# Two weight sums of a pair made by the transfers that load them, and 26 feed-forward pairs in the wide form

## The chip, the cores and the metric

The kernel runs on one core of a Trainium2 chip. The metric is the time of one execution in device microseconds; several runs are given by their median.

## The reference

One decoder layer on 512 tokens of width 1024, all in float32: a SwiGLU feed-forward, a mixer that merges dilated window attention with a linear recurrence, and a second SwiGLU feed-forward. Root-mean-square norms stand around each. What the change touches are the products of the inputs with the gate and up weights of the feed-forwards, and with weights of the mixer's input projection.

```python
def swiglu(x, w_gate, w_up, w_down):
    return (jax.nn.silu(x @ w_gate) * (x @ w_up)) @ w_down

for l in range(DEPTH):                       # DEPTH = 1
    f = swiglu(rms_norm(h, ffn1_norm_pre[l]), ffn1_w_gate[l], ffn1_w_up[l], ffn1_w_down[l])
    h = h + 0.5 * rms_norm(f, ffn1_norm_post[l])
    u = rms_norm(h, mix_norm_pre[l])
    proj = u @ w_in[l]
    q, k, v, xr, yr, gl = jnp.split(proj, splits, axis=-1)
    ...
    h = h + rms_norm(merged @ w_out[l], mix_norm_post[l])
    f = swiglu(rms_norm(h, ffn2_norm_pre[l]), ffn2_w_gate[l], ffn2_w_up[l], ffn2_w_down[l])
    h = h + 0.5 * rms_norm(f, ffn2_norm_post[l])
```

The feed-forward width is 2816, which is 22 blocks of 128 columns. There are 12 attention heads of width 128, in three groups of four.

## The kernel before

**Split products.** TensorE takes its operands in a reduced float format (`F32R`). The kernel keeps the precision by splitting each operand into a high part, rounded, and a low part, the rest, and by adding three products: high by high, high by low, low by high. `split` (L302, L303) makes both parts of a tile: a copy on ScalarE writes the high part, a subtraction on VectorE the low one. Weights arrive in `raw` tiles (128 x 1024, four buffers) by transfers on the SP queue, in one fixed stream (`stream_plan`); their split parts go to `w8` tiles (four buffers) and `w4` tiles (two).

**Pairs.** Two blocks of 128 output columns, gate and up of one block f in a feed-forward or a query and a key block in attention, make a pair. A pair has four quarters of weights: g0, g1 (gate, first and second half of the 1024 rows) and u0, u1 (up). It is computed with seven products instead of eight, in the manner of Strassen and Winograd, over the two halves of the rows and the two halves of the tokens. The input's forms are made once per stage (`x_forms`, `forms_of`). The weights' forms are made per pair by `w_forms`: four adds of 128 x 512 on VectorE (L691, L692, L693, L696) and four splits, three of 1024 columns (tiles a, b, c) and one of 512 (d). The sums are

- s2 = u0 + u1 (for p5), s1 = u0 + u1 + g0 (for p6), u0 + g0 (for p7) and u0 + u1 + g0 + g1 (for p3); g0, g1 and u1 themselves serve p1, p2 and p4.

In this kernel tile a holds p1 and p2, tile b (from the tile `s12`, tag `s`, two buffers) p6 and p5, tile c p7 and p4.

**Three ways to run the seven products.** Each product is a sum over four blocks of 128 rows.

- `seven_on` (narrow, L729 to L731): three matmuls of 256 columns for each block, high by high, high by low, low by high, all into one 256-column area. Partial results are copied by ScalarE from one bank to the next and added by VectorE from the banks.
- `seven` is a variant of it for the first pairs of a feed-forward.
- `seven_wide` (L779, L780): the high weight is loaded once and multiplied with high and low input side by side, 512 columns; the low weight then multiplies the high input, 256 columns, into the second half. The result stands in two halves of a bank. Moves between banks (`move`, L784) are 512 wide, a result is made by `fold` (a copy of one half by ScalarE, L790, and an add by VectorE, L792) or `sum_of` (two adds, L800, L802).

The order of the seven is p1, p5, p6, p2, p7, p3, p4 in `seven_on` and `seven_wide`. Before the change the feed-forwards use `seven` and, from block 5 on (`FIRST_ON`), `seven_on`; attention's 12 query and key pairs, its four gate pairs and three pairs of the recurrence use `seven_wide`.

**Order of the work.** In a feed-forward the first blocks are done without the scheme; then `ffn_order` lists, for each block f, the preparation of the weights of f + 1 (`prep`, one pair ahead), of down weights (`prepd`), the products of f (`prod`), and one step of the down products of an earlier group of blocks (`down7`, L1043 to L1045, with its results carried to the sums by ScalarE, L1032 and L1048). In attention `pair_of` prepares the next pair when a pair begins; three pairs make the queries and keys of a head, then `attend` works on the head before. The framework fixes one order of instructions for each engine; `tc.high_priority` moves an instruction ahead in it by a number of places (weights by `AHEAD` = 100, results in PSUM by `EVAC` = 200). Each engine runs its list in order and waits at the first instruction that is not ready. POOL, the fourth engine, only starts a few transfers of its own queue (gains, residuals).

Of the kernel before, what the change touches and what calls it, by code (L numbers as in the profile page):

```python
# [10 lines left out]
F32 = mybir.dt.float32  # L11
F32R = mybir.dt.float32r
AF = mybir.ActivationFunctionType
ALU = mybir.AluOpType
AX = mybir.AxisListType

P = 128
T = 512
D = 1024
KC = D // P  # L20
NF = 22
FF_PARTS = ((0, 4), (4, 8), (8, 12), (12, 16), (16, 22))
NSTD = {1: 6, 2: 3}

SEVEN = range(4)
STEPS_AT = {1: ((6, 7, 7, 8), range(9, 13), range(13, 17), range(17, 21)),
# [4 lines left out]
HB = 256  # L31
RAW_W = 1024
NEG = -1.0e30

FIRST_ON = {1: 5, 2: 5}
AHEAD = 100
# [29 lines left out]
def ffn_order(n):  # L66

    order = [("std", f) for f in range(NSTD[n])]  # L70
    after = {}
# [3 lines left out]
    ready = False  # L75
    for f in range(NSTD[n], NF):
        if not ready:
# [106 lines left out]
def hybrid_layer(ctx: ExitStack, tc: tile.TileContext, xT: bass.AP, xN: bass.AP, wst: bass.AP,  # L184
                 first: bass.AP, rows: bass.AP, consts: bass.AP, bias: bass.AP, out: bass.AP):
    nc = tc.nc
    DVE, ACT, PE = nc.vector, nc.scalar, nc.tensor
# [3 lines left out]
    wpool = ctx.enter_context(tc.tile_pool(name="wpool", bufs=4))  # L191
# [39 lines left out]
    groups = stream_groups()  # L231
    state = {"g": 0, "i": 0, "off": 0, "raw": None, "ahead": AHEAD, "split": None}
# [21 lines left out]
    def raw_two(key, dst=None):  # L254

        return [raw_of(key + (n,), None if dst is None else dst[:, i * RAW_W:(i + 1) * RAW_W])
                for i, n in enumerate(("lo", "hi"))]
# [10 lines left out]
    def w8():  # L268
        return wpool.tile([P, 2, 1024], F32R, name="w8", tag="w8", bufs=4)

    def w4():
        return wpool.tile([P, 2, 512], F32R, name="w4", tag="w4", bufs=2)
# [28 lines left out]
    def split(dh, dl, src):  # L301
        state["split"] = ACT.activation(dh, src, AF.Copy).ins  # L302
        state["low"] = DVE.tensor_sub(dl, src, dh.bitcast(F32)).ins  # L303

    def acc_ps():
        return psum.tile([P, T], F32, name="acc", tag="acc", bufs=5)
# [4 lines left out]
    def tmp(name):  # L311
        return tpool.tile([P, T], F32, name=name, tag="t")
# [17 lines left out]
    def gemm(ps, wt, x, sl=slice(0, T), ks=None):  # L330
        n = x.n
        a, b = k128(wt[0], n), k128(wt[1], n)
        for k in ks or range(n):
            mm3(ps, a[:, k, :], b[:, k, :], x.hi[k][:, sl], x.lo[k][:, sl], k == 0, k == n - 1)
# [17 lines left out]
    HALVES = (slice(0, HB), slice(HB, T))  # L352
# [328 lines left out]

    spool = [None]

    def w_forms(key):

        with tc.high_priority(offset=AHEAD):
            ur, gr = raw_two(key)
            u0, u1, g0, g1 = (r[:, i * 512:(i + 1) * 512] for r in (ur, gr) for i in range(2))
            s12 = spool[0].tile([P, 2, 512], F32, name="s12", tag="s", bufs=2)
            s1, s2 = s12[:, 0, :], s12[:, 1, :]  # L690
            DVE.tensor_add(s2, u0, u1)  # L691
            DVE.tensor_add(s1, s2, g0)  # L692
            DVE.tensor_add(u0, u0, g0)  # L693
            a, b, c, d = w8(), w8(), w8(), w4()
            split(a[:, 0, :], a[:, 1, :], gr)
            DVE.tensor_add(g1, s1, g1)  # L696
            split(b[:, 0, :], b[:, 1, :], s12.rearrange("p s c -> p (s c)"))
            split(c[:, 0, :], c[:, 1, :], ur)
            split(d[:, 0, :], d[:, 1, :], g1)
            lo, hi = slice(0, 512), slice(512, 1024)  # L700
            return {"p1": a[:, :, lo], "p2": a[:, :, hi], "p6": b[:, :, lo], "p5": b[:, :, hi],
                    "p7": c[:, :, lo], "p4": c[:, :, hi], "p3": d}
# [122 lines left out]
    def seven(t, w, z, g, u):  # L825


        b, y = acc_ps()[:, :HB], acc_ps()[:, :HB]

        def product(p, ps, start):  # L830
            seventh(t, w, p, ps, start)

        def copy(ps):
            c = tpool.tile([P, HB], F32, name="c", tag="c", bufs=CB)
            with tc.high_priority(offset=EVAC):
                ACT.activation(c, ps, AF.Copy)
            return c

        def sum_of(dst, ps, c):
            with tc.high_priority(offset=EVAC):  # L840
                DVE.tensor_add(dst, ps, c)

        product("p1", b, True)
        c1 = copy(b)
        product("p2", y, True)
        sum_of(g[0], y, c1)
        product("p6", b, False)
        c6 = copy(b)
        product("p5", z, True)
        c5 = copy(z)  # L850
        product("p7", b, False)
        c7 = copy(b)
        sum_of(u[1], c7, c5)
        product("p4", y, True)
        sum_of(u[0], y, c7)
        product("p3", z, False)
        sum_of(g[1], z, c6)

    def ffn(n, x, r, forms_x, apool, pss):
        t, steps = forms_x  # L860
# [81 lines left out]

        def prod(f, w):
            g, u = tmp("g"), tmp("u")
            if f >= FIRST_ON[n]:
                lo, hi = HALVES

                def g1(z, c6):
                    with tc.high_priority(offset=EVAC):
                        DVE.tensor_add(g[:, hi], z, c6)  # L950
                    ACT.activation(g[:, hi], g[:, hi], AF.Silu)

                def u1(b, c5):
                    with tc.high_priority(offset=EVAC):
                        DVE.tensor_add(u[:, hi], b, c5)

                def u0(v):
                    def put(dst, view):
                        for q, (h, src) in enumerate(zip(HALVES, (v, u[:, hi]))):
                            DVE.scalar_tensor_tensor(dst[:, q] if len(dst.shape) == 3 else dst[:, h], g[:, h], -1.0,  # L960
                                                     src, op0=ALU.mult, op1=ALU.mult)
                    into(f, put)

                seven_on(t, w, lambda y: ACT.activation(g[:, lo], y, AF.Silu), g1, u0, u1)
                return
            seven(t, w, acc_ps()[:, :HB], [g[:, h] for h in HALVES], [u[:, h] for h in HALVES])
            ACT.activation(g, g, AF.Silu)
            into(f, lambda dst, v: DVE.scalar_tensor_tensor(dst, v(g), -1.0, v(u), op0=ALU.mult, op1=ALU.mult))

# [53 lines left out]
        def groups(i):  # L1023
            return [(p, k) for p in SEVEN_STEPS[i] for k in range(2)]
# [41 lines left out]

        keys = [(w, n, i) for i in range(NSTD[n]) for w in ("gate", "up")]
        forms = {}
        for ev in ffn_order(n):
            if ev[0] == "std":  # L1070
                j = ev[1]
                while len(pss) < 2 * j + 2:
                    pss.append(acc_ps())
                    gemm(pss[-1], fetch(keys[len(pss) - 1]), x)
                with tc.high_priority(offset=EVAC if j == NSTD[n] - 1 else 0):
                    std_out(pss[2 * j], pss[2 * j + 1], j)

                for step in steps[j:] if j == min(NSTD[n], 4) - 1 else steps[j:j + 1]:
                    step()
            elif ev[0] == "prep":  # L1080
                forms[ev[1]] = w_forms(("gu", n, ev[1]))
            elif ev[0] == "prepd":
                forms[ev[1:]] = d_forms(*ev[1:])
            elif ev[0] == "seeds":
                for g in groups(ev[2])[:3]:
                    seed(ev[1], *g)
            elif ev[0] == "down7":
                down7(*ev[1:], forms.pop(ev[1:]))
            else:
                prod(ev[1], forms.pop(ev[1]))  # L1090
        a = len(FF_PARTS) - 1
# [32 lines left out]
    for k in range(KC):  # L1124
        wh, wl, raw = wts[k]
# [77 lines left out]
    with ExitStack() as mx:  # L1203
# [38 lines left out]
        def values_two(steps, then):  # L1242
# [78 lines left out]
            for j in range(2):  # L1321
# [4 lines left out]
        t, steps = forms_of(lambda i, j: Form(lambda s, k: um_t[2 * i + k // 2][:, s, k % 2, HALVES[j]]),  # L1326
                            apool, False, rec_half)
        values_first()
        pairs = [[(g * 4 + hd, 12 + g * 4 + hd) for g in range(NG)] for hd in range(NH)]
        order = [("pair",) + p for ps in pairs for p in ps] + [("pair", 52 + c, 53 + c) for c in range(0, KC, 2)]  # L1330
        forms = {}
# [8 lines left out]
        def pair_of(key):  # L1340

            i = order.index(key)
            if i + 1 < len(order):
                forms[order[i + 1]] = w_forms(order[i + 1])
            return forms.pop(key)

        def qk(hd):
# [147 lines left out]
        for c in range(0, KC, 2):  # L1495
            g, u = tmp("g"), tmp("u")
            seven_wide(t, pair_of(("pair", 52 + c, 53 + c)), [g[:, h] for h in HALVES], [u[:, h] for h in HALVES],
                       then=gate)
# [10 lines left out]
    with ExitStack() as mx:  # L1509
# [183 lines left out]
        for c in range(KC):  # L1693
            if c < 3:
                ps = pss[c]
            else:
# [17 lines left out]
                 {(1, 3): lambda: (bd2.turn(0), bd2.turn(1))})  # L1714
    keys = [(w, 2, i) for i in range(NSTD[2]) for w in ("gate", "up")]
    pss = gemm_first(keys[:NFIRST], u2, [spare(ap2)["tx"]],
# [5 lines left out]
    grow5, _ = gains(ap2, 4)  # L1722
# [138 lines left out]
```

## Time and profile before

| | |
|---|---|
| median of 3 runs | 1210.02 us (1209.67 to 1210.19) |
| the profiled execution | 1209.61 us, of which 1207.8 us are its span |
| first feed-forward | to about 330 us |
| attention, with queries and keys | about 405 to 600 us |
| second feed-forward, its pairs | about 898 to 1170 us |
| granted TensorE clock | 0.999 |

The profile is one execution. A row of a group gives line, engine, operation, what is written and read, the count, and the busy time with the mean duration of one. A row of a timeline gives start, duration, engine and line. Durations of neighbours on one engine overlap at their ends, so the distance from start to start is what one costs in a full queue. A row of the windows gives, for a stretch of time, how long each engine was busy, with the number of its instructions in parentheses, then the granted TensorE clock, the busy share of the 16 DMA engines and GB/s.

### The profile page before, as it was taken

The numbers are of one execution on the slowest core, as the hardware profiler recorded it, in microseconds if no ns is written. First come the engines' busy times: TensorE is split into PE (matmuls) and PEld (weight loads), VectorE is DVE, ScalarE is ACT, GpSimd is POOL, SyncE is SP. The second block draws the span as 40 slices with busy tenths as digits, with TensorE's granted clock in tenths as the row PEclk, the third lists the DMA queues.
The fourth block names the chain that finished last, engine by engine and source line by source line (L and its number), as shares of the span: only waits on it lengthen the run. The fifth ranks groups of instructions, "written<-read, shape, count | busy, mean of one in ns | idle before, by whom it ended". The sixth has DMA issues, their size and how long they took to land.

```text
span 1207.8 us, 18850 instructions
## 1 busy us (share of the span) xinstructions
PE 1198.6 (99%) x7222; PEld 1070.1 (89%) x7222; DVE 1033.3 (86%) x1626; ACT 831.8 (69%) x1447; POOL 26.1 (2%) x51
## 2 busy tenths in 40 slices
PE   9999999999999999999999999999999999999997
PEld 8889999999888888888888888888899999999996
DVE  7999888989689899999868999774799888889964
ACT  6566787887566576777736988734566687778763
POOL 0000000000011000000000000000100000000000
PEclk9999999999999999999999999999999999999999
DMA  7224343434725232222323532235443333333441
GB/s 267 88 92 139 120 139 109 137 117 150 250 106 154 71 101 91 89 87 80 122 67 110 176 121 88 88 107 189 140 142 121 121 125 117 128 120 126 125 173 70
DMA packets 45819, 149.77 MB, mean 124 GB/s; under 512 B 5152, under 2 KB 8608, under 8 KB 45728
## 3 DMA queue, kind: packets, MB, share of 16 engines
q1 hardware_dynamic: 38160, 131.09, 32.9%
q0 software_dynamic: 7280, 17.30, 4.3%
q8 instruction: 56, 0.92, 0.3%
q14 instruction: 35, 0.29, 0.1%
q10 hardware_dynamic: 288, 0.17, 0.0%
HBM read 138.06 MB, written 6.29 MB: 120 GB/s over the span
## 4 chain that ended last, share of the span: by engine, by line
PE 92%; DVE 4%; DMA 2%; ACT 1%; issue 1%; DVEq 0%; ACTq 0%
PE acc L779 10%; PE acc L729 9%; PE acc L731 9%; PE acc L730 9%; PE acc L315 7%; PE acc L317 7%; PE acc L316 7%; PE acc L780 5%; PE aux L1043 4%; PE aux L1044 4%; PE aux L1045 4%; PE acc L433 2%; PE acc L432 2%; PE acc L431 2%; DVE w L303 2%; DMA raw<-in_w 2%
## 5 line engine op out<-in xcount | busy, mean ns | idle before, releaser
L303 DVE TENSOR_TENSOR w<-raw,w 128x1024 fp32r<-128x1024 f32 (+1 forms) x272 | 296.9, 1097 | 32.2 <-ACT w L302 31.4
L302 ACT ACTIVATE w<-raw 128x1024 fp32r<-128x1024 f32 (+1 forms) x272 | 259.5, 958 | 90.0 <-PE acc L317 48.2
L729 PE MATMUL acc<-big,w 128*128 128x256 f32 x860 | 243.6, 283 | 0.0
L731 PE MATMUL acc<-big,w 128*128 128x256 f32 x860 | 243.4, 283 | 0.0
L730 PE MATMUL acc<-big,w 128*128 128x256 f32 x860 | 243.3, 283 | 0.0
L729 PEld LDWEIGHTS acc<-big,w 128*128 128x128 f32 x860 | 164.8, 192 | 1.8
L730 PEld LDWEIGHTS acc<-big,w 128*128 128x128 f32 x860 | 164.8, 192 | 1.5
L731 PEld LDWEIGHTS acc<-big,w 128*128 128x128 f32 x860 | 164.8, 192 | 0.0
L779 PE MATMUL acc<-big,w 128*128 128x512 f32 x380 | 136.5, 398 | 0.0
L780 PE MATMUL acc<-big,w 128*128 128x256 f32 x380 | 107.5, 283 | 0.0
L1043 PE MATMUL aux<-w,xf 128*128 128x512 f32 x224 | 87.3, 392 | 0.6 <-ACT w L302 0.6
L1044 PE MATMUL aux<-w,xf 128*128 128x512 f32 x224 | 87.5, 391 | 0.0
L1045 PE MATMUL aux<-w,xf 128*128 128x512 f32 x224 | 87.2, 389 | 0.0
L779 PEld LDWEIGHTS acc<-big,w 128*128 128x128 f32 x380 | 71.4, 188 | 16.0 <-ACT acc L784 0.2
L780 PEld LDWEIGHTS acc<-big,w 128*128 128x128 f32 x380 | 71.7, 189 | 0.3
L303 DVE TENSOR_TENSOR w<-s,w 128x1024 fp32r<-128x1024 f32 x51 | 62.2, 1220 | 3.2 <-ACT w L302 2.7
L315 PE MATMUL acc<-xf,w 128*128 128x512 f32 (+1 forms) x168 | 59.2, 354 | 0.0
L316 PE MATMUL acc<-xf,w 128*128 128x512 f32 (+1 forms) x168 | 58.7, 350 | 0.0
L317 PE MATMUL acc<-xf,w 128*128 128x512 f32 (+1 forms) x168 | 58.5, 349 | 0.0
L302 ACT ACTIVATE w<-s 128x1024 fp32r<-128x1024 f32 x51 | 53.9, 1057 | 6.2 <-PE acc L731 3.0
L779 PE MATMUL acc<-rb,w 128*128 128x512 f32 x152 | 55.5, 397 | 0.0
L743 ACT ACTIVATE c<-acc 128x256 f32<-128x256 f32 x68 | 25.8, 383 | 35.3 <-PE acc L731 35.3
(458 smaller groups left out, 2919.5 us busy)
## 6 DMA issues: line engine op xcount, KB each, us to landing
raw<-in_w SPq DMA_DIRECT2D x232, 512.0 KB, 3.5
big<-xf POOLq DMA_DIRECT2D x6, 512.0 KB, 3.3
gains<-in_rows POOLq DMA_DIRECT2D x5, 512.0 KB, 5.4
h<-in_x SPq DMA_DIRECT2D x8, 256.0 KB, 5.1
h<-in_xn POOLq DMA_DIRECT2D x4, 512.0 KB, 6.7
kept_m<-h POOLq DMA_DIRECT2D x4, 512.0 KB, 2.9
vals<-in_w SPq DMA_DIRECT2D x4, 512.0 KB, 6.0
h<-kept_m POOLq DMA_DIRECT2D x4, 512.0 KB, 6.2
```

The source lines that it names most:

```text
L302: state["split"] = ACT.activation(dh, src, AF.Copy).ins
L303: state["low"] = DVE.tensor_sub(dl, src, dh.bitcast(F32)).ins
L315: PE.matmul(ps, wh, xh, start=first, stop=False)
L316: PE.matmul(ps, wh, xl, start=False, stop=False)
L317: PE.matmul(ps, wl, xh, start=False, stop=last)
L729: PE.matmul(ps, wh, xh, start=start and k == 0, stop=False, skip_group_check=True)
L730: PE.matmul(ps, wh, xl, start=False, stop=False, skip_group_check=True)
L731: PE.matmul(ps, wl, xh, start=False, stop=k == 3, skip_group_check=True)
L779: PE.matmul(part, wh, at(BOTH, k), start=start and k == 0, stop=False, skip_group_check=True)
L780: PE.matmul(cross, wl, at(0, k), start=False, stop=k == 3, skip_group_check=True)
L1043: PE.matmul(ps, xh, wh, start=first and j == 0, stop=False, skip_group_check=True)
L1044: PE.matmul(ps, xh, wl, start=False, stop=False, skip_group_check=True)
```

## The change

Two things are changed.

1. For 45 pairs (blocks 8 to 21 of the first feed-forward, 5 to 21 of the second, and all pairs of attention but the first two) two of the four sums are not added by VectorE. `sums_ahead` starts them on the POOL queue a pair ahead: one transfer writes u0 twice into a tile `s12`, a second one adds u1 to the first copy and g0 to the second, in the transfer itself (`accum_op`). So the tile holds u0 + u1 and u0 + g0. `w_forms_summed` then loads g0 and g1 into one `raw` tile and u1 alone into the second half of another, and makes the other two sums with two adds (L716, L719 of the changed kernel). The tiles are grouped anew: b now holds p5 and p7, c holds p6 and p4; a and d stay.
2. Blocks 10 to 21 of the first feed-forward and 8 to 21 of the second, 26 pairs, are run by `seven_wide` instead of `seven_on`.

The diff, cut to its core:

```diff
+WIDE = {1: range(10, NF), 2: range(8, NF)}
+SUMMED = {1: 8, 2: 5}
...
-    def w_forms(key):
+    def rows_of(key, o, *dims):
+        return bass.AP(tensor=wst.tensor, offset=wst.offset + starts[key + ("lo",)] + o,
+                       ap=[[RAW_W, P], *dims, [1, T]])
+
+    def sums_ahead(key):
+        with tc.high_priority(offset=AHEAD):
+            s = spool[0].tile([P, 2, T], F32, name="s12", tag="s", bufs=2)
+            nc.gpsimd.dma_start(s, rows_of(key, 0, [0, 2]))
+            nc.gpsimd.dma_start(s, rows_of(key, T, [P * RAW_W - T, 2]), accum_op=ALU.add)
+            summed[key] = s
+
+    def w_forms_summed(key):
+        s = summed.pop(key)
+        with tc.high_priority(offset=AHEAD):
...
+            gr, ur = (wpool.tile([P, RAW_W], F32, name="raw", tag="raw", bufs=4) for _ in range(2))
+            nc.sync.dma_start(gr, rows_of(key, P * RAW_W, [T, 2]))
+            nc.sync.dma_start(ur[:, T:], rows_of(key, T))
...
+            a, b, c, d = w8(), w8(), w8(), w4()
+            split(a[:, 0, :], a[:, 1, :], gr)
+            DVE.tensor_add(ur[:, :T], s[:, 0, :], gr[:, :T])
+            split(b[:, 0, :], b[:, 1, :], s.rearrange("p s c -> p (s c)"))
+            split(c[:, 0, :], c[:, 1, :], ur)
+            DVE.tensor_add(gr[:, T:], ur[:, :T], gr[:, T:])
+            split(d[:, 0, :], d[:, 1, :], gr[:, T:])
+            lo, hi = slice(0, T), slice(T, D)
+            return {"p1": a[:, :, lo], "p2": a[:, :, hi], "p5": b[:, :, lo], "p7": b[:, :, hi],
+                    "p6": c[:, :, lo], "p4": c[:, :, hi], "p3": d}
+
+    def w_forms(key, then=None):
+        if key in summed:
+            w = w_forms_summed(key)
+        else:
+            w = w_forms_made(key)
+        if then:
+            sums_ahead(then)
+        return w
...
             g, u = tmp("g"), tmp("u")
-            if f >= FIRST_ON[n]:
+            if f in WIDE[n]:
+                seven_wide(t, w, *([x[:, h] for h in HALVES] for x in (g, u)))
+            elif f >= FIRST_ON[n]:
...
-                forms[ev[1]] = w_forms(("gu", n, ev[1]))
+                f = ev[1]
+                forms[f] = w_forms(("gu", n, f), ("gu", n, f + 1) if SUMMED[n] <= f + 1 < NF else None)
...
-                forms[order[i + 1]] = w_forms(order[i + 1])
+                forms[order[i + 1]] = w_forms(order[i + 1], order[i + 2] if 2 <= i + 2 < len(order) else None)
```

More of the change, by code (lines that the diff above doesn't have):

```diff
@@ L682, in hybrid_layer, with w_forms_made @@
     spool = [None]
-    def w_forms(key):
+    starts, summed, end = {}, {}, 0
+    for grp in groups[1:]:
+        starts[grp[0][0]] = end
+        end += (grp[-1][1] + grp[-1][2]) * P
+    def rows_of(key, o, *dims):
[10 more added lines that the diff above has]
+        with tc.high_priority(offset=AHEAD):
+            g = state["g"]
+            assert state["i"] == 0 and [k for k, _, _ in groups[g] + groups[g + 1]] == [key + ("lo",), key + ("hi",)]
+            assert state["off"] == starts[key + ("lo",)]
+            gr, ur = (wpool.tile([P, RAW_W], F32, name="raw", tag="raw", bufs=4) for _ in range(2))
+            nc.sync.dma_start(gr, rows_of(key, P * RAW_W, [T, 2]))
+            nc.sync.dma_start(ur[:, T:], rows_of(key, T))
+            state["g"], state["off"] = g + 2, state["off"] + 2 * P * RAW_W
+            a, b, c, d = w8(), w8(), w8(), w4()
[16 more added lines that the diff above has]
+        return w
+    def w_forms_made(key):
         with tc.high_priority(offset=AHEAD):
@@ L965, in prod @@
                 return
-            seven(t, w, acc_ps()[:, :HB], [g[:, h] for h in HALVES], [u[:, h] for h in HALVES])
+            else:
+                seven(t, w, acc_ps()[:, :HB], [g[:, h] for h in HALVES], [u[:, h] for h in HALVES])
             ACT.activation(g, g, AF.Silu)
```

## The prediction

> **What bounds the kernel now.** I read the page first: busy time, then the chain that ended last.
>
> ```profile
> span 1207.8 us, 18850 instructions
> ...
> PE 1198.6 (99%) x7222; PEld 1070.1 (89%) x7222; DVE 1033.3 (86%) x1626; ACT 831.8 (69%) x1447; POOL 26.1 (2%) x51
> ...
> PE 92%; DVE 4%; DMA 2%; ACT 1%; issue 1%; DVEq 0%; ACTq 0%
> ```
>
> TensorE (PE) sets the end; VectorE (DVE) is second, POOL idle. So an edit gains only what it takes off TensorE, and loses what it makes TensorE wait. The next view is the windows of six stretches.
>
> ```profile
> core 0: us, PE busy (x) PEld busy (x) DVE busy (x) ACT busy (x) POOL busy (x), PEclk, DMA share, GB/s
> 106.07:116.14 10.07, 10.07 (x85) 10.07 (x84) 10.00 (x14) 6.30 (x11) 0.00 (x0) 1.00 0.50 158
> 623.18:642.78 19.60, 19.60 (x114) 17.06 (x112) 15.26 (x27) 15.43 (x24) 0.00 (x0) 1.00 0.28 88
> 485.08:501.46 16.38, 16.38 (x96) 14.23 (x95) 15.35 (x37) 12.59 (x26) 0.00 (x0) 1.00 0.29 93
> 165.51:224.95 59.44, 59.44 (x421) 56.08 (x420) 51.25 (x69) 47.39 (x81) 0.00 (x0) 1.00 0.38 125
> 968.53:1028.60 60.07, 59.86 (x421) 56.19 (x420) 50.88 (x68) 46.84 (x82) 0.00 (x0) 1.00 0.38 123
> 410.00:600.00 190.00, 189.34 (x1167) 167.70 (x1167) 178.68 (x399) 134.92 (x301) 0.00 (x0) 1.00 0.29 93
> ```
>
> Row 1 is one feed-forward pair in the narrow form (84 weight loads), row 2 two pairs in the wide form (112), both without a gap: 10.07 against 9.80 us a pair. Row 3 is wide pairs in attention: 93 matmuls begin in 16.38 us (the row counts three more at its edges), 9.86 us per 56. Rows 4 and 5 are four pairs of each feed-forward with their down products: TensorE full, VectorE at 86 and 85%, ScalarE (ACT) at 80 and 78%. Row 6 is attention: VectorE at 94%, with 11.3 us left idle.
>
> Engines overlap the ends of instructions, so what one costs in a full queue is the distance between starts, read from timelines of VectorE and ScalarE:
>
> ```profile
> 286.50 1.22 DVE L303 TENSOR_TENSOR w<-raw,w 128x1024 fp32r<-128x1024 f32 x1
> 287.64 0.68 DVE L692 TENSOR_TENSOR s<-s,raw 128x512 f32<-128x512 f32 x1
> 288.24 0.68 DVE L693 TENSOR_TENSOR raw<-raw 128x512 f32<-128x512 f32 x1
> 288.84 0.41 DVE L960 SCALAR_TENSOR_TENSOR u<-g,acc 128x256 f32<-128x256 f32 x1
> 289.18 0.42 DVE L960 SCALAR_TENSOR_TENSOR u<-g,u 128x256 f32<-128x256 f32 x1
> ...
> 225.99 1.05 ACT L302 ACTIVATE w<-raw 128x1024 fp32r<-128x1024 f32 x1
> 226.93 0.37 ACT L743 ACTIVATE acc<-acc 128x256 f32<-128x256 f32 x1
> ...
> 634.79 0.37 ACT L790 ACTIVATE ge<-acc 128x256 f32<-128x256 f32 x1
> 635.05 0.59 ACT L784 ACTIVATE acc<-acc 128x512 f32<-128x512 f32 x1
> 635.57 0.62 ACT L302 ACTIVATE w<-raw 128x512 fp32r<-128x512 f32 x1
> 636.08 0.62 ACT L1596 ACTIVATE ge<-ge 128x512 f32<-128x512 f32 x1
> ```
>
> VectorE: 1.14 us for 1024 columns, 0.60 for 512, 0.34 for 256. ScalarE: 0.94, 0.52 and 0.26.
>
> **Part 1: 26 pairs go wide.** The wide form runs one 512-column and one 256-column matmul where the narrow one runs three of 256: 768 columns either way, with one weight load fewer. The gain on TensorE is 10.07 - 9.80 = 0.27 us a pair, 26 x 0.27 = 7.0 us. The Trainium skill ("TensorE: Matmul & The Clock Gate", "Back-to-back issue gap") has N/2.4 + 2.5 ns between matmuls, by which a pair would save 0.07 us and 26 pairs 1.8 us, an estimate of mine; rows 1 and 2 differ by 0.27, and I go by them.
>
> The price is paid off TensorE. VectorE: the narrow form has four instructions of 256 (1.36 us), the wide one eight of 256 and a product of 512 (3.32): +1.96 a pair. ScalarE: four copies and two Silu of 256 (1.56) become three moves of 512, four copies of 256 and a Silu of 512 (3.12): +1.56.
>
> **Part 2: sums by transfer.** Two adds of 512 leave VectorE per pair, -1.2 us, in 45 pairs: 31 in the feed-forwards and 14 in attention. With both parts, a wide feed-forward pair costs VectorE +0.76 and ScalarE +1.56. For the four pairs of row 4: VectorE 51.25 + 3.0 = 54.3 and ScalarE 47.4 + 6.2 = 53.6 of 59.44 - 1.1 = 58.3 us, 93 and 92%. Both still fit, so neither becomes the bound on average.
>
> What can still hold TensorE are waits inside a pair. Three moves (first product to the bank of the third, third to the fifth, fifth to the seventh) have one product of 1.40 us as cover; ScalarE needs 0.52 of it, and the last matmul's drain 0.28:
>
> ```profile
> 623.77 0.28 PE L780 MATMUL acc<-big,w 128*128 128x256 f32 x1
> 623.89 0.40 PE L779 MATMUL acc<-big,w 128*128 128x512 f32 x1
> 624.12 0.28 PE L780 MATMUL acc<-big,w 128*128 128x256 f32 x1
> ```
>
> That leaves 0.6 us. A split of 0.94 begun just before the move is due makes TensorE wait 0.34. Bounds per pair are 0 (rows of 623, ScalarE at 79%) and 1.0 (all three moves hit). Attention's wide pairs at 77% ScalarE and 94% VectorE lose 0.06 (9.86 against 9.80); at 92 and 93% I take twice that, 0.12: 26 x 0.12 = +3.1 us.
>
> A second wait: the pair's third weight tile now serves products 3 and 7 (p6, p4) where it served 5 and 7 (p7, p4), so it is due two products, 2.8 us, earlier. Its VectorE split and the start of its pair, now:
>
> ```profile
> 239.89 1.22 DVE L303 TENSOR_TENSOR w<-raw,w 128x1024 fp32r<-128x1024 f32 x1
> ...
> 240.49 0.28 PE L729 MATMUL acc<-big,w 128*128 128x256 f32 x1
> ```
>
> It ends at 241.11, and product 5 begins 4 x 1.44 = 5.8 us after 240.49, at 246.2: 5.1 us of slack, which become 2.3. VectorE's work up to it stays (four adds and two splits of 1024, 4.7 us, against two adds and three splits, 4.6). I cost it at nothing; ScalarE or VectorE later by over 2.3 us would use the cover up.
>
> **Part 3: the transfers themselves.** Each sum is two POOL transfers of 512 KB, the second adding into what the first wrote and waiting for it. Together they take D. No accumulating transfer is in this trace. What is: a single POOL load in a window of its own, and others as pairs or from SBUF (answers on the window 1139 to 1145 and on two lines).
>
> ```profile
> q0 software_dynamic: 144, 0.52, 27.0%
> ...
> gains<-in_rows POOLq DMA_DIRECT2D x1, 512.0 KB, 3.8
> ...
> L655 POOL DMA_DIRECT2D big<-xf x6: 740/749/762, 860.5 to 882.1; - x6
> ...
> DMA to landing us min/median/max: 3.1/3.3/5.8
> ...
> h<-kept_m POOLq DMA_DIRECT2D x4, 512.0 KB, 6.2
> ```
>
> The load lands in 3.8 us, of which its packets take 27% of 6 us = 1.6. From below D is 2 x 3.1 = 6.2; from above, at the rate of transfers that share the engines, 2 x 6.2 = 12.4. I take the lone load, 3.8, and for the add the same with its packets' time doubled (it must read its destination too), 3.8 + 1.6 = 5.4: D = 9.2. The Trainium skill points both ways: "DMA: Bandwidth & Descriptors" ("Anatomy of one DMA") fits 2.0 us + bytes/436e3, 3.2 us each and 6.4 for two, while "Collectives: The Full Stack" ("The bandwidth ceiling") has an adding transfer at half the rate of a copy, since it reads two sources. No run here shows which.
>
> Who waits? There are two sum buffers. A transfer may begin when the split two sums earlier has freed its buffer, and VectorE's first add of the pair stands behind its landing, with everything that is queued after it. I counted, in the changed kernel's order of instructions, VectorE's work (at the distances above) or TensorE's products that it must follow, whichever is longer, from one to the other. In the feed-forwards this gap is 14.1 to 28.5 us for 31 sums: D is covered. In attention, where three pairs follow each other at 9.8 us, the 14 gaps are 8.3, 7.8, 7.8, 9.8, 6.7, 8.4, 8.7, 12.1, 6.6, 16.7, 6.4, 13.1, 9.7, 9.9. The shortest holds four PSUM sums (1.36), two splits (2.28), three folds (1.02), a reduction and two adds (1.8): 6.4. At D = 9.2 eight adds wait, 13 us together, three of them 2.5 to 2.8. VectorE has 11.3 us idle in attention and gets 14 x 1.2 = 16.8, so on the whole it can afford that; forms late by those three would hold TensorE between 0 and 8 us. I take +1.0. Against it, attention's pairs can gain at most what they lose now, 14 x 0.06 = -0.8.
>
> Costed at nothing: 45 x 0.79 MB = 35 MB more through the DMA engines (at 1.6 us for 0.52 MB, 110 us of all engines, 9% of the span, beside a share of 0.29 to 0.38 in rows 4 to 6; a load that lands later for it delays a split, which has the 2.3 us); 90 POOL instructions of 0.75 us on an idle engine (gains, residual loads and stores queue behind the last sum of their stage only); the SP queue keeps its count, one load of each summed pair being half as long.
>
> **Sum.** -7.0 + 3.1 - 0.8 + 1.0 = -3.7 us against the profiled execution, whose time is 1209.6 (span 1207.8 and 1.8 around it): 1205.9. The median of the runs is 0.4 above that execution: 1206.3. A change under 0.2%, 2.4 us, is about what a measurement here cannot tell from none.
>
> **Rivals.**
>
> *The sums come late in attention* (slower). At D = 12.4 the adds wait 46.6 us in all; VectorE has 28.1 to give, so 18.5 stay: 1210.0 - 7.0 + 3.1 + 18.5 = 1224.6. It decides from D = 11.3, where 6 us are left over and the whole is 2 us slower. For it: SP's loads run beside these transfers, and its rows are cut to 2 KB. Against it: the lone load's 3.8.
>
> *The sums come in time everywhere* (faster): D up to 7.5, which the 6.4 of the page's fit would give. No wait in attention, and moves as free as in row 2: 1210.0 - 7.0 - 0.8 = 1202.2.
>
> *ScalarE's moves hold TensorE.* At 92% in a fixed order, two of three moves come behind a split: 26 x 0.68 = 17.7, and 1210.0 - 7.0 + 17.7 = 1220.7; from 0.27 a pair the gain is gone. Against it: ScalarE has 4.7 us to spare in four pairs.
>
> *Wide saves nothing in the feed-forwards*, TensorE being paced by columns alone: 1210.0 + 3.1 - 0.8 = 1212.3 at worst, 1208 if the moves are free. By the page on TensorE it would be 1.8 us. Rows 1 and 2 speak against it.
>
> **Chances.** Forecast 0.38, late sums 0.23, sums in time 0.23, moves 0.10, nothing saved 0.04, else 0.02. Faster by over 0.2%: 0.30 of the forecast (its terms reach 1209 at the worst of the 8 us) and 0.23: 0.53. Slower: late sums 0.23, moves 0.08, else 0.02: 0.33. Within: 0.08 of the forecast, 0.04 nothing saved, 0.02 moves: 0.14. The range goes from 1199.5 (the fast case less 2.7 us, for waits on VectorE and DMA, 6% of the chain, that may go with the adds) to 1222 (D = 12.2), leaving out the far part of late sums and little else; the forecast's own case is 1202 to 1211.
>
> **What would show it.** The wide pairs of the feed-forwards at 9.8 to 9.95 us, without idle of more than 0.2 before a third, fifth or seventh product. VectorE's add behind the POOL transfer waiting on DMA in attention for about 13 us in all and in the feed-forwards not at all; the adding transfer landing in about 5.4 us, the plain one in 3.8. VectorE and ScalarE at 92 to 93% in rows like 4. Wrong if the adding transfer takes over 7.5 us, or if pairs in the feed-forwards take longer than 10.07.

## The result, and the profile after

The changed kernel takes 1251.05 us (median of 4 runs, 1249.49 to 1253.24) against 1210.11 us of the kernel before: a ratio of 1.034, with a 95% interval of 1.0322 to 1.0358. It is slower by 41 us, and the prediction said 1206.3. The profiled execution took 1251.06 us. First the page: span, busy time, chain, and the transfers' landing times.

```profile
span 1249.3 us, 17779 instructions
...
PE 1209.0 (97%) x6494; PEld 1037.4 (83%) x6494; DVE 1032.6 (83%) x1666; ACT 866.8 (69%) x1499; POOL 114.2 (9%) x141
...
PE 63%; issue 12%; DVE 10%; DMA 7%; ACT 7%; POOL 1%; DVEq 0%; POOLq 0%; ACTq 0%
...
raw<-in_w SPq DMA_DIRECT2D x187, 512.0 KB, 4.3
s<-in_w POOLq DMA_DIRECT2D x90, 512.0 KB, 5.8
```

TensorE was 92% of the chain and is now 63%; transfers, VectorE and ScalarE have taken its place, with 12% of "issue", time in which the engine waited for nothing that the profile shows. TensorE's idle time in the span grew from 9.2 to 40.3 us. Its busy time grew by 10.4 us, at a granted clock of 0.990 instead of 0.999. The windows of after: one wide feed-forward pair, four pairs in each feed-forward, and attention; last, attention in the kernel before.

```profile
core 0: us, PE busy (x) PEld busy (x) DVE busy (x) ACT busy (x) POOL busy (x), PEclk, DMA share, GB/s
261.60:271.48 9.88, 9.88 (x58) 8.57 (x57) 8.45 (x15) 7.90 (x15) 1.21 (x1) 1.00 0.80 220
170.98:230.25 59.27, 58.93 (x310) 50.03 (x310) 54.45 (x81) 52.16 (x90) 8.13 (x9) 1.00 0.66 178
1053.37:1113.48 60.11, 59.23 (x309) 50.05 (x308) 54.51 (x81) 52.92 (x91) 8.55 (x9) 1.00 0.64 176
412.92:633.36 220.44, 202.03 (x1190) 175.69 (x1188) 167.39 (x376) 139.31 (x305) 26.62 (x27) 0.97 0.51 133
```
```profile
407.36:601.19 193.83, 193.17 (x1189) 171.05 (x1188) 181.86 (x403) 137.91 (x305) 0.00 (x0) 1.00 0.30 96
```

Attention took 193.83 us and takes 220.44: +26.6. TensorE sits idle for 18.4 us of the stage, 17.7 more than before; the other 8.9 us are busy time that became longer, at a granted clock of 0.97. By the moments at which TensorE begins the stages, the first feed-forward lost 5.3 us (its end moved from 310.00 to 315.33) and the second one 9.1 (270.1 to 279.2). The three make 5.3 + 26.6 + 9.1 = 41.

**Attention.** POOL's timeline (start, duration; in brackets the idle time before it and what ended it) and VectorE's, from the same 20 us:

```profile
425.63 0.74 POOL L699 DMA_DIRECT2D s<-in_w  x1 [7.91 <-DVE qk L843]
430.50 1.21 POOL L700 DMA_DIRECT2D s<-in_w  x1 [4.13 <-DMA s<-in_w]
439.25 0.74 POOL L699 DMA_DIRECT2D s<-in_w  x1 [7.54 <-DVE qk L843]
```
```profile
422.96 0.69 DVE L716 TENSOR_TENSOR raw<-s,raw 128x512 f32<-128x512 f32 x1 [4.93 <-DMA s<-in_w]
423.57 0.42 DVE L843 TENSOR_TENSOR c<-acc,c 128x256 f32<-128x256 f32 x1
423.91 1.22 DVE L305 TENSOR_TENSOR w<-s,w 128x1024 fp32r<-128x1024 f32 x1
...
436.68 0.69 DVE L716 TENSOR_TENSOR raw<-s,raw 128x512 f32<-128x512 f32 x1 [4.83 <-DMA s<-in_w]
```

The copy (L699) begins at 425.63, the adding transfer (L700) is issued at 430.50, and the add that needs it (L716) starts at 436.68: D is 11.05 us. The copy in turn began only when VectorE had made the split of 423.91 (`w<-s`), 0.5 us after its end (the bracket names `qk`, the instruction that VectorE runs next; the split is the one that reads the buffer). This split stands close behind the previous add, which had waited for the previous sum. In the order of instructions the split behind an add is that of the pair before it, and it frees the buffer for the sum after. So it is a closed loop: add, split, copy, adding transfer, add; one round takes 436.68 - 422.96 = 13.7 us, where pairs followed each other at 9.8. VectorE's waits in attention name it (total, times, longest):

```profile
DVE raw L716 <- DMA s<-in_w: 31.8, 10, 4.9
```

**Feed-forwards.** Landing times in the first feed-forward: first all 63 loads of the weight stream before the change; then, after it, the 32 loads that do not belong to summed pairs; then the adding transfer there and (last) in attention:

```profile
DMA to landing us min/median/max: 3.3/3.5/7.3
```
```profile
who waited for it (us, times):
  DVE sum L1054: 7.4, 4
  DVE raw L1049: 4.3, 3
...
DMA to landing us min/median/max: 3.2/4.7/9.8
```
```profile
DMA to landing us min/median/max: 5.7/7.7/9.3
```
```profile
DMA to landing us min/median/max: 6.0/6.3/6.6
```

These loads land a third later, up to 9.8 us after their issue (with those of the summed pairs, some of which are half as long, the median of all is 4.5 us). Those who wait are the adds that form the down weights (L1049, L1054), which before the change waited for no load in this stretch. A piece of the chain of waits shows how it reaches TensorE (start, duration, what): a load, the add behind it, ScalarE's work for the down products, and the matmul, which had waited 2.0 us:

```profile
94.01 6.56 DMA raw<-in_w
...
100.67 1.23 DVE sum L1054
...
103.62 0.49 ACT facc L1102
...
104.16 0.50 PE aux L1097
```

The 36 matmuls of the down products around it take 12.1 us instead of 8.2. In the second feed-forward these adds wait 14.2 us (0.9 before). There 4 us go at its start (the first 168 matmuls take 24.1 us instead of 20.2). The first sum's copy begins when the split of an input form (`big<-ts`, a tile of the same tag `s`) has freed its buffer; the sum is there 12.7 us later, and VectorE has stood at the add for 3.8 us:

```profile
933.24 0.71 POOL L699 DMA_DIRECT2D s<-in_w  x1 [17.29 <-DVE big L305]
...
937.75 1.23 POOL L700 DMA_DIRECT2D s<-in_w  x1 [0.47 <-DMA s<-in_w]
```
```profile
946.00 0.69 DVE L716 TENSOR_TENSOR raw<-s,raw 128x512 f32<-128x512 f32 x1 [3.81 <-DMA s<-in_w]
```

### The profile page after: what moved, and what is told of

Read it like the earlier page. It is cut to its first block, busy times and chain, and to the rows that moved or that the text cites. A ratio compares the mean times of both kernels' runs of the same rounds, so it can differ in the third digit from the quotient of the medians.

```text
span 1249.3 us, 17779 instructions
## 1 busy us (share of the span) xinstructions
PE 1209.0 (97%) x6494; PEld 1037.4 (83%) x6494; DVE 1032.6 (83%) x1666; ACT 866.8 (69%) x1499; POOL 114.2 (9%) x141
## 4 chain that ended last, share of the span: by engine, by line
PE 63%; issue 12%; DVE 10%; DMA 7%; ACT 7%; POOL 1%; DVEq 0%; POOLq 0%; ACTq 0%
PE acc L830 13%; PE acc L317 6%; PE acc L319 6%; PE acc L318 6%; PE acc L831 6%; DVE w L305 4%; DMA raw<-in_w 4%; DMA s<-in_w 3%; ACT w L304 3%; PE aux L1097 3%; PE aux L1098 2%; PE aux L1099 2%; PE acc L433 2%; PE acc L435 2%; PE acc L434 2%
## 5 line engine op out<-in xcount | busy, mean ns | idle before, releaser
L830 PE MATMUL acc<-big,w 128*128 128x512 f32 x1004 | 363.0, 401 | 9.8 <-DVE qk L853 6.4
L831 PE MATMUL acc<-big,w 128*128 128x256 f32 x1004 | 283.4, 283 | 0.0
L830 PEld LDWEIGHTS acc<-big,w 128*128 128x128 f32 x1004 | 189.8, 189 | 57.3 <-issue 7.4
L831 PEld LDWEIGHTS acc<-big,w 128*128 128x128 f32 x1004 | 190.7, 190 | 1.6
L835 ACT ACTIVATE acc<-acc 128x512 f32<-128x512 f32 x135 | 79.1, 586 | 31.9 <-PE acc L831 28.7
L1097 PE MATMUL aux<-w,xf 128*128 128x512 f32 x224 | 89.0, 398 | 6.8 <-ACT facc L1102 3.8
L1098 PE MATMUL aux<-w,xf 128*128 128x512 f32 x224 | 88.2, 394 | 0.0
L1099 PE MATMUL aux<-w,xf 128*128 128x512 f32 x224 | 87.9, 393 | 0.0
L699 POOL DMA_DIRECT2D s<-in_w x45 | 33.7, 749 | 492.6 <-DVE w L305 248.4
L700 POOL DMA_DIRECT2D s<-in_w x45 | 54.4, 1208 | 188.8 <-DMA s<-in_w 188.8
L780 PE MATMUL acc<-big,w 128*128 128x256 f32 x236 | 67.6, 287 | 2.4 <-ACT c L887 2.4
L781 PE MATMUL acc<-big,w 128*128 128x256 f32 x236 | 67.4, 286 | 0.0
L782 PE MATMUL acc<-big,w 128*128 128x256 f32 x236 | 67.3, 285 | 0.0
L716 DVE TENSOR_TENSOR raw<-s,raw 128x512 f32<-128x512 f32 x45 | 31.0, 688 | 40.2 <-DMA s<-in_w 35.6
```

Source lines behind the costliest of these rows:

```text
L780: PE.matmul(ps, wh, xh, start=start and k == 0, stop=False, skip_group_check=True)
L830: PE.matmul(part, wh, at(BOTH, k), start=start and k == 0, stop=False, skip_group_check=True)
L831: PE.matmul(cross, wl, at(0, k), start=False, stop=k == 3, skip_group_check=True)
L835: return ACT.activation(dst, src, AF.Copy).ins
L1097: PE.matmul(ps, xh, wh, start=first and j == 0, stop=False, skip_group_check=True)
L1098: PE.matmul(ps, xh, wl, start=False, stop=False, skip_group_check=True)
```

## The experiments

The theory from these views: attention's loss is the sums' time D in the closed loop; in the feed-forwards the transfers delay the loads of the weight stream, and the wide pairs' gain is lost to that. Rivals: the bytes themselves delay, whatever the transfer does; the wide form costs by itself; the new order of the loads costs. The results together (medians; the ratio is to runs of the kernel before on the same chip; the stages are differences in the profiled execution to the kernel before, in us; the executions of some runs with sums lie several us apart, up to 11 us in "feed-forward sums alone, adding made a copy", so a stage's figure is that of one execution):

| run | us | ratio, 95% interval | 1st f.-f. | attention | 2nd f.-f. |
|---|---|---|---|---|---|
| the change | 1251.05 | 1.0322 to 1.0358 | +5.3 | +26.6 | +9.1 |
| no sums in attention | 1223.11 | 1.0095 to 1.0129 | +6.8 | -0.2 | +8.7 |
| wide pairs alone | 1221.7 | 1.0085 to 1.0115 | +6.3 | +0.1 | +5.9 |
| feed-forward sums alone, narrow | 1254.61 | 1.0349 to 1.0384 | +17.3 | -0.1 | +27.9 |
| the change, adding made a copy | 1229.82 | 1.0143 to 1.0186 | +2.2 | +12.4 | +3.5 |
| wide in every second place | 1208.41 | 0.9982 to 1.0 | +0.6 | -0.3 | -1.0 |
| feed-forward sums alone, adding made a copy | 1231.17 | 1.0138 to 1.0209 | +10.2 | -0.5 | +14.0 |
| the change, first copy only | 1217.07 | 1.0048 to 1.0075 | -0.3 | +6.9 | 0.0 |
| feed-forward sums alone, first copy only | 1216.21 | 1.0043 to 1.007 | +4.6 | -0.1 | +1.9 |
| the change, third buffer in attention | 1234.65 | 1.019 to 1.0225 | +3.7 | +6.0 | +8.9 |
| wide without the last three | 1211.98 | 1.001 to 1.0029 | -0.7 | -0.2 | +2.6 |
| feed-forward sums alone, without eight | 1221.0 | 1.0077 to 1.0107 | +3.8 | -0.1 | +6.8 |
| wide and feed-forward sums, without eight | 1218.57 | 1.0049 to 1.0083 | +4.0 | +0.1 | +5.7 |

**No sums in attention.**

```diff
-                forms[order[i + 1]] = w_forms(order[i + 1], order[i + 2] if 2 <= i + 2 < len(order) else None)
+                forms[order[i + 1]] = w_forms(order[i + 1])
```

> The changed kernel without the sums by transfer in attention (its 14 pairs get their sums from VectorE as before); the feed-forwards keep wide pairs and sums. Theory 'late sums': in attention a sum takes 13 to 14 us from the begin of its copy to the landing of its adding transfer, and the pairs follow each other faster, so all of the attention stage's 26.6 us are waits for them: 1251.0 - 26.6 = 1224.5 us, and the attention stage is again 193.8 us. Rival 'spread': the feed-forwards' changes move what follows too (splits and loads left behind), and attention keeps some of its loss: above 1230 us.

1223.11 us, and attention is as long as before. The stages add up: attention's 26.6 us are its sums. (The 13 to 14 us for a sum are those of the feed-forwards; in attention it took 11.)

**Wide pairs alone.** As above, and:

```diff
-SUMMED = {1: 8, 2: 5}
+SUMMED = {1: NF, 2: NF}
```

> Only the 26 wide pairs of the feed-forwards; no sum by transfer anywhere. Theory 'late sums': the wide pairs that nothing disturbed took 9.88 us in the trace of after against 10.07 for a narrow pair, so 26 of them save 26 x 0.19 = 4.9 us: 1205 us. Rival 'the wide form saves nothing' (their mean in the first feed-forward of after was 10.07): 1210 us. Rival 'ScalarE's moves hold TensorE': pairs of 10.3 to 10.6 us, 1216 to 1224 us.

1221.7 us, within the third theory's numbers but not by its mechanism. TensorE's waits name a bank that VectorE empties late (`sum_of`), twice, 5 us each; and in the windows the stretch ahead of the second wait (1093 to 1151) has VectorE at 57.19 of 58 us:

```profile
PE acc L830 <- DVE u L853: 10.3, 2, 5.5
PE aux L1175 <- DVE eps L230: 1.1, 1, 1.1
PE acc L830 <- ACT acc L835: 1.0, 3, 0.5
```
```profile
1093.00:1151.00 58.00, 58.00 (x306) 49.06 (x304) 57.19 (x84) 49.09 (x83) 0.54 (x1) 1.00 0.41 136
```

So VectorE, with 2 us more per wide pair and no sum taken off it, falls behind and is the bound at the ends of both feed-forwards. Ahead of the result that TensorE waits for, VectorE's list there also has the adds that merge the down products (L1113 to L1116, 1.13 us each), which come only at these ends. The waits named for ScalarE's moves (L835) make 1.0 us.

**Feed-forward sums alone, narrow pairs.** `WIDE = {1: (), 2: ()}` and no sums in attention.

> Only the feed-forwards' sums by transfer, narrow pairs as before, attention as before. The two feed-forwards together lost 14.4 us in after. Theory 'late sums and loads': the transfers delay the two loads of a pair and the first sums, and a wide pair saves 0.19 us: the sums alone cost 14.4 + 4.9 = 19 us, 1229 us; if the wide pairs save nothing, 1224 us. Rival 'the wide form is the cost': the sums lie beside other work, 1210 us.

1254.61 us: the sums alone cost 45 us, more than the whole change, and far more than I expected. The chain of waits around one of its stalls (start, duration, what):

```profile
204.44 1.24 DVE w L305
205.67 0.02 issue
205.69 7.84 DMA raw<-in_w
213.53 0.03 issue
213.55 0.02 DVEq L1049
213.57 0.04 issue
213.62 1.23 DVE raw L1049
```

A split frees one of the four `raw` buffers, the load of a down block begins in it at once and takes 7.84 us beside an adding transfer issued at 204.7, and VectorE stands at the add of that block. This recurs in every group of four pairs; in the second feed-forward alone:

```profile
DVE raw L1049 <- DMA raw<-in_w: 30.6, 4, 8.1
```

**The change with the adding transfer as a copy.** In `sums_ahead`:

```diff
-            nc.gpsimd.dma_start(s, rows_of(key, T, [P * RAW_W - T, 2]), accum_op=ALU.add)
+            nc.gpsimd.dma_start(s, rows_of(key, T, [P * RAW_W - T, 2]))
```

> The changed kernel with the adding transfer made a plain copy of the same 512 KB (the addition is left out of the sums). Theory 'the adding transfer is the price': after's plain copy took 4.3 us and 0.75 us of GpSimd, its adding one 7.5 and 1.2; a sum is then ready after some 10 us instead of 13.6, the waits in attention fall to about a third (the gaps of the order give 20 us of waits at 10.0 and 61 at 13.6, of which 26.6 were seen): 1251 - 18 = 1233 us, less if the feed-forwards' loads land earlier too. Rival 'traffic': the bytes are what delays (52% of the DMA engines' time in attention), and with as many bytes it is 1247 to 1251 us.

1229.82 us: with as many bytes, 21 of the 41 us are gone, 14 of them in attention, where the second transfer now lands in 4.4 us (median) instead of 6.3 and the waits for sums are half. A sum takes 9.2 us there (median):

```profile
DVE raw L716 <- DMA s<-in_w: 15.8, 7, 3.5
```

**Wide in every second place.** No sums; `WIDE = {1: range(10, NF, 2), 2: range(8, NF, 2)}`.

> No sum by transfer; wide pairs only in every second one of the 26 places (13 pairs). Theory 'VectorE overrun': a wide pair that nothing holds takes 9.88 us against 10.07, and the 12.4 us that 26 of them lost came from VectorE, which they load with 2 us more a pair, falling behind at a few places; with half of them it keeps up: 13 x 0.19 = 2.5 us saved, 1206.8 us. Rival 'each wide pair costs': 12.4 / 26 = 0.48 us each, 1215.5 us.

1208.41 us in 11 runs, ratio 0.9991: 1.4 us faster, at the edge of its interval. VectorE keeps up. Six of the 13 wide pairs took 9.88 us, the others 10.05 to 10.6, their moves a little late. It is the fastest version of all, and the only one not slower than the kernel before.

**Feed-forward sums alone, the adding transfer as a copy, and left out.** Both are the run with narrow pairs, with the edit above, and with that line deleted.

> Sums by transfer in the feed-forwards alone, narrow pairs, attention as before, and the adding transfer a plain copy of as many bytes (the addition is left out). Theory 'the adding transfer holds the loads': the down blocks' loads, for which VectorE waited 52 us, land in 4 to 5 us again instead of 7.8, and some 15 of the 45 us remain: 1224 us. Rival 'order of the loads': the summed pair's loads and splits come in an order in which the four load buffers come round too late, whatever the transfer takes: 1245 us or more.

> Sums by transfer in the feed-forwards alone, narrow pairs, attention as before, the adding transfer left out. Theory 'the adding transfer holds the loads': 1209 to 1213 us. Rival 'order of the loads': 1240 us or more, since the order of the instructions is that of the run with the sums in the feed-forwards alone.

1231.17 and 1216.21 us. Of 45 us, 21 stay with two copies and 6.4 with one; the order of VectorE's, TensorE's and SP's instructions is the same in all three, but for nine of VectorE's 1564 places in the last. The theory expected 15 and at most 3: the time of the transfers sets most of it, and the order, with the one copy left, at most 6.4 us.

**The change with the first copy only.** The adding line is deleted.

> The changed kernel with the adding transfer left out altogether (the sums' tile holds the copied blocks alone): half the added bytes, and a sum 'ready' 5 us after its begin. Theory 'late sums': every gap in attention is longer than that (6.4 us at least), so attention is as long as before (+0), and the wide pairs, with VectorE relieved, save 26 x 0.19 = 4.9 us: 1204 us. Rival 'order of the loads': the feed-forwards lose as much as in the run without attention's sums (13.8 us): 1223 us.

1217.07 us. Neither number: the feed-forwards are back at the time of before (not 4.9 us under it), but attention keeps 6.9 us, with 5.1 us of waits for a transfer that lands in 4.3 (in this kernel the orders of VectorE and TensorE differ in places from the change's, so the 6.9 us aren't the copy's alone):

```profile
DVE raw L715 <- DMA s<-in_w: 5.1, 3, 1.9
```

**A third buffer in attention.** Three buffers for the tag `s` there, `CB = 4`, `tpool` with three buffers, and:

```diff
-                forms[order[i + 1]] = w_forms(order[i + 1], order[i + 2] if 2 <= i + 2 < len(order) else None)
+                forms[order[i + 1]] = w_forms(order[i + 1], order[i + 3] if i + 3 < len(order) else None)
```

> The changed kernel with three buffers for the sums in attention instead of two, and each sum begun one pair earlier. Room for the third is made by four instead of six buffers of the tiles c and three instead of four of the tiles t. Theory 'closed loop': with two buffers a copy waits for the split that frees its buffer, this split stands behind VectorE's add, which waits for the sum before, so sums of 11 us follow each other without overlap, one in 13.7 us; with a third buffer the waits for sums (31.8 us in attention) go and 1251 - 26.7 = 1224 us are left, up to 1230 if loads land later. Rival 'traffic': the bytes delay, whenever they are begun: 1240 to 1251 us.

1234.65 us. The loop is open: the adding transfer still lands in 6.3 us (median), the waits for sums fall from 31.8 to 2.6, and attention's loss from 26.6 to 6.0.

```profile
DVE raw L718 <- DMA s<-in_w: 2.6, 1, 2.6
```

Where the rest of attention's 6.0 us comes from stays open. The total is above the 1224 to 1230 since the part between attention and the second feed-forward took 5.7 us more: TensorE waits there once, 2.8 us for a split of the recurrence on ScalarE (`rb`, at 798.6), and then runs at a clock of 0.50 for 5.8 us, which is worth another 2.9. Some tiles were made fewer for the third buffer, but no run shows that as the cause of this wait.

**Wide without the last three.** No sums; `WIDE = {1: range(10, NF - 3), 2: range(8, NF - 3)}`.

> No sums by transfer; wide pairs as in the change except the last three of each feed-forward (20 pairs). Theory 'VectorE overrun at the end': nearly all of the 12.4 us that 26 wide pairs lost were two waits of TensorE for VectorE of 5 us each, in the last pairs of the two feed-forwards, with the half clock after them; without these pairs 20 x 0.19 = 3.8 us are saved less 1 to 2 for single late moves: 1207.5 us. Rival 'each wide pair costs' 0.48: 1219 us.

1211.98 us, between the two. The 5 us waits are gone; VectorE's backlog outlives the wide pairs and holds a narrow one for 2.0 us at the end of the second feed-forward.

**Without the sums that meet the third down block.** `MEET` holds, for each group, the block f at which that down block is prepared; the edit is made in the run with narrow pairs, then in that with wide ones.

```diff
+MEET = {n: [list(STEPS_AT[n][a])[2] for a in SEVEN] for n in (1, 2)}
...
-                forms[f] = w_forms(("gu", n, f), ("gu", n, f + 1) if SUMMED[n] <= f + 1 < NF else None)
+                forms[f] = w_forms(("gu", n, f), ("gu", n, f + 1) if SUMMED[n] <= f + 1 < NF and f not in MEET[n] else None)
```

> As the run with sums in the feed-forwards alone and narrow pairs, but without the sums whose transfers are under way when the third down block of a group is loaded: 23 of 31 sums are left. Theory 'the meeting': VectorE's add of that block waited 7 to 8 us for its load in each group of four pairs, and that is the 45 us; without these eight sums 1209.8 + 0 to 5 = 1210 to 1215 us. Rival 'spread': each sum costs its share, 45 x 23 / 31 = 33 us: 1243 us.

> The 26 wide pairs with the sums of the feed-forwards, without attention's sums and without the same eight sums. Theory 'the meeting': the run with all 31 sums took 1223.1 us, with 16.7 us of VectorE waiting for the third down blocks' loads; without them the wide pairs' 4.9 us come out less some 3 for other late loads: 1208 us. Rival 'spread': 23 / 31 of 13.8 us stay, or VectorE, which gets eight sums back, falls behind again: 1218 to 1220 us.

With narrow pairs 1221.0 us: eight of 31 sums carried 34 of the 45 us. 11 stay, above what the meeting alone allows, with 26 us of VectorE's waits at the same add (49 before). With wide pairs 1218.57 us, as the rival said: the waits at that add fell from 16.7 to 9.2 us, and only 4.9 of the 13.8 us went. Why wide pairs meet these loads less harshly than narrow ones (13.8 us for wide pairs and sums together, 45 for sums alone) was not settled. Part of it is the clock: 0.988 with narrow pairs against 0.998, some 13 us of the difference (an estimate from these shares and the spans).

## Why the prediction was wrong, point by point

**Which step failed.** Four terms did, and the largest was the credit for VectorE's spare time. At the measured D of 11.1 us the fourteen gaps that the prediction counted give 32.0 us of waits, and 31.8 were measured: the count was right. But the prediction let VectorE pay 28.1 us of waits out of its idle time and saved adds. It paid 5 at most (31.8 less 26.6): VectorE's busy time in attention did fall by 14.5 us (181.86 to 167.39), and the stage became longer by 26.6 all the same. The run with the adding transfer as a copy tests the credit by itself, since there a sum takes 9.2 us in attention, just what the prediction took for D. The waits were 15.8 us, near the 13 forecast, and attention lost 12.4 us where the prediction had +1.0 - 0.8 and let TensorE be held 8 at the worst. Spare time helps where a wait stands once; here each wait holds the split that starts the next sum, so the round of 13.7 us, and not VectorE's load, became attention's pace. The third buffer shows it: same transfers, same adds, 20.6 us less.

**D** was the second: 9.2 taken, 11.05 measured. The adding transfer took 6.3 us to land in attention where 5.4 was taken (POOL's 1.21 us for issuing it included), the copy 4.3 where 3.8 was, and some 0.4 us lie between the copy's landing and the adding transfer's begin. With 9.2 attention lost 12.4 us, so the other 14.2 of its 26.6 come with the longer D. The bounds, 6.2 to 12.4, held in attention; in the feed-forwards a sum took 13 us (median). The two rules of the Trainium skill that were weighed there can now be read: the fit of "DMA: Bandwidth & Descriptors" ("Anatomy of one DMA"), 3.2 us for one such transfer, is below the 4.3 measured; half the rate for an adding one, which "Collectives: The Full Stack" ("The bandwidth ceiling") states for collectives, is the right direction, with 6.3 against 4.3 us from issue to landing.

**The bytes costed at nothing** were the third, in the feed-forwards: the median of all the loads rose from 3.5 to 4.5 us in the first, and the down blocks' adds, which the prediction did not look at, wait at loads that begin only when a buffer comes free. The 35 MB were weighed against the DMA engines' average share, and not against the moment at which a load has to land. How long the transfers take counts as much as the bytes: the two feed-forwards lost 14.4 us together, 5.7 with as many bytes and no addition, and nothing with the first copy only. The gap counted for the feed-forwards, 14.1 us and more, failed for one sum, the first of the second feed-forward: from the copy's begin at 933.24 VectorE reached the add in 9 us, less than the 12.7 of the sum, and this cost 4 us.

**The wide pairs.** Where nothing holds it the form is worth what was said: 9.88 us, inside the 9.8 to 9.95 forecast, a saving of 0.19 us. The loads of VectorE and ScalarE in four pairs were forecast at 93 and 92% and are 92 and 88% (54.45 and 52.16 of 59.27). But the term for the moves, 0.12 us a pair, was the fourth that failed: the 26 wide pairs of the change average 10.16 us (10.07 in the first feed-forward, 10.23 in the second) where 9.92 was forecast, so nothing is saved and 26 x 0.24 = 6.2 us are missing. Five of the twelve in the first feed-forward are held for 0.2 to 0.6 us right before the third, fifth or seventh product, where a move is due. The mechanism is the prediction's own, a split on ScalarE begun just ahead of the move; here in a pair that took 10.58 us:

```profile
159.48 1.06 ACT L304 ACTIVATE w<-raw 128x1024 fp32r<-128x1024 f32 x1
160.43 0.60 ACT L835 ACTIVATE acc<-acc 128x512 f32<-128x512 f32 x1
```

Late loads are not needed for this. With the first copy only, where the feed-forwards are as long as before, the mean is 10.11 us; with wide pairs alone, leaving out the two pairs of the 5 us waits, 10.02. The average load also hid that VectorE, without sums, was at 99% ahead of the stall.

**The rivals.** "The sums come late in attention" named the right place and chain, but asked for D above 11.3 and priced it at 18.5 us with 12.4; it came at 11.1 with 26.6, since its price takes the same 28.1 us off. "ScalarE's moves" named the right place for the wide pairs, but with 0.68 us a pair; they average 0.36 over the free 9.80. The signs that the prediction set as proof of error appeared: the adding transfer takes over 7.5 us in the feed-forwards (7.7 in the first, 6.3 in attention), and pairs of 10.3 to 11.6 us stand in the second feed-forward.

Of the 44.7 us between forecast and result attention has 26.4 and the feed-forwards have 18.3: 6.2 from the wide pairs, and the rest from the late loads and that one sum.

## What to carry to other kernels

A wait in an in-order queue is not paid from that engine's idle time when what stands behind it starts the next thing waited for: look for the loop and compare its round with the pace of the work. Where it was longer here, a further buffer took 20.6 of attention's 26.6 us away and a faster transfer 14.2. Before moving work from an engine to transfers, find the loads that start only when a buffer comes free; added transfers cost there, at single moments, whatever the average share says. And an engine near 95% can have stretches at 99%, so half of a change that loads it can be better than all (1208.4 against 1221.7 us).

## What the hardware showed that was not expected

After a wait TensorE often runs at half speed for some microseconds. The windows of the run with wide pairs alone: a stretch ahead of the first of its two long waits, the wait, what follows it, and full speed again; then the second wait and what follows it (PEclk is the column ahead of the last two).

```profile
293.90:298.00 4.10, 4.10 (x22) 3.38 (x20) 4.10 (x5) 3.21 (x5) 0.00 (x0) 1.00 0.61 247
298.00:303.00 5.00, 0.22 (x2) 0.00 (x0) 5.00 (x8) 1.35 (x4) 1.05 (x2) 0.74 0.81 244
303.05:306.37 3.32, 3.32 (x10) 2.83 (x11) 3.32 (x6) 2.25 (x5) 0.12 (x1) 0.50 0.67 258
307.60:316.00 8.40, 8.40 (x47) 7.22 (x46) 5.26 (x8) 5.68 (x10) 0.00 (x0) 1.00 0.60 195
1151.00:1156.50 5.50, 0.06 (x1) 0.00 (x0) 5.50 (x8) 1.16 (x4) 0.00 (x0) 0.75 0.55 191
1156.60:1160.70 4.10, 4.10 (x13) 3.52 (x14) 4.10 (x8) 2.42 (x6) 0.00 (x0) 0.52 0.00 0
```

A wait of 5 us is followed by 3.3 to 4.1 us at a clock of 0.50 to 0.52, so it costs about 7. The Trainium skill ("TensorE: Matmul & The Clock Gate", "HAM oscillation — how this bites in real kernels") warns of gaps above some 3.4 us; these two waits agree. But shorter waits did it too. In the changed kernel a wait of 2.0 us is followed, 1.5 us later, by 3.3 us at 0.50:

```profile
102.10:104.20 2.10, 0.09 (x2) 0.04 (x1) 1.91 (x5) 1.94 (x4) 0.00 (x0) 1.00 0.00 0
105.70:109.00 3.30, 3.30 (x9) 2.61 (x8) 3.27 (x5) 3.30 (x7) 0.74 (x1) 0.50 0.01 1
```

Of the six waits of 2.0 to 2.6 us in that trace five have such a stretch behind them, and none of the six of 1.0 to 1.8 us has. In attention three of these stretches, 13.4 us together, are worth 6.7 of the 8.9 us by which its busy time grew (an estimate, half of them). In the kernel before, the clock was 0.999 and no wait was longer than 1.1 us.
